# Hybrid trunk: evictions ahead of renewals in some chains, decay passes behind the cast, the dt sums one product later

## The chip, the cores and the metric

One core of one Trainium2 chip. The metric is the device time of one execution in microseconds; "before" is the median of three runs, 2637.45 us (2635.89 to 2637.7).

The engines are named as in the profile: PE (TensorE, matmuls; PEld its weight loads), DVE (VectorE), ACT (ScalarE), POOL (GpSimd) and SP (SyncE, which issues the DMAs).

## The reference

One layer of a hybrid trunk on x of 2048 tokens by 1024 channels, all in float32:

```
h = rmsnorm(x);  proj = h @ w_in          # u_b, u_c, u_h, z, xbc, dt_raw
y_a = u_b * conv3(u_c * u_h)              # short convolution mixer
xbc = silu(conv4(xbc));  dt = softplus(dt_raw + dt_bias)
y_b = chunked state-space scan over dt, a, B, C, xs   (+ d_skip * xs)
y_b = grouped rmsnorm(y_b * silu(z))
x = x + concat(y_a, y_b) @ w_out
x = x + square(relu(rmsnorm(x) @ w_up)) @ w_down;  out = rmsnorm(x)
```

In the scan each of 16 heads (two groups of eight) has within a chunk a matrix of decays exp(min(a_cum[l] - a_cum[s], 0)), which weighs the products of B and C below the diagonal.

## The kernel before

**Products.** The input projection, the MLP's up projection and its down projection are done in `chain` (L250): a two-by-two block product by seven smaller products in place of eight, in the order b11, t1, t2, b21, t3, b22, t4 (`PRODUCTS`). Each operand is held as a high and a low part of reduced width, so that each pair of blocks is three matmuls of 128x128 by 128x512 (L281 to L283). A chain with four block pairs per product has 12 matmuls per product. The accumulators lie in banks of PSUM: px and py take turns over three banks, pw has one of its own. A bank is free again when the eviction of its product has run, so a product whose bank is not yet read out waits. After b11 ACT copies px into pw (L288), and b21 adds to it.

**Evictions.** `evict` is handed in by the user of the chain. In the input projection (`Proj.pair`) s5 and s2 are copied by ACT (L746), added to later products by DVE (L749), and t4's product goes through Silu on ACT (L784); z rows are then stored to sz_d (L775, L785). In the MLP (`Mlp.pair`) they are copies, adds (L897) and squared relu (L900, L901). In the down projection (`Mlp.down`) DVE adds the product to acc (L1051).

**Renewals.** The operands of a chain are blocks uh and ul, four places of four tiles. Where the next chain needs other blocks they are renewed while the old chain runs: `fetch` or `refill` load the raw block from DRAM (rb, rh, nb), and `settle` makes the high part on ACT (L352) and the low part on DVE (L353), one place after each of t1, b21, b22 and t4. This happens in the chains of the pair z6 (the last of the first half of tokens), at the boundary of the MLP's halves and its end, and in the steps of the down projection. Weights for the next chain are loaded by SP (wraw, three buffers), combined into s12 and s34 on DVE (L214, L237), and split into whi on ACT (L100) and wlo on DVE (L101).

**Down projection.** `STEPS` (L1197): step 0 has one group of four blocks, step 1 one group of two, step 2 two groups of one and three, all later steps four blocks. The weights of step n+1 are loaded and split during step n. Before step 0 the last sums of the MLP are stored (t4, L885).

**Scan.** 32 chunks of 128 tokens by group. `front` (L1278) prepares a chunk: PE transposes xd (ptx) and B (ptb); ACT copies xtok (L1291) and btok; DVE scales xtok by decays (stmp, L1301); ACT casts the high part of it (L1303) and DVE makes the low part (L1308). Eight Relu passes (L1306, one per head) and one Exp (L1307) on ACT turn the loaded rows dec into decays. `back` then runs the products st, yo and yd. The first 16 chunks run beside the second half of the input projection with one buffer of each tile, the other 16 beside the output projection (matmuls pm, L113 to L115) with two, so that there the rows of the next chunk are loaded before the present one is through its front.

**dt.** `dt_part` (L631) is a generator that is advanced between products: pd (L640), then pt and the softplus, then after two more yields the cumulative sums pc (L677, L678), then pr and the stores of rd_d and dt_d, which the scan loads.

**Order.** Each engine runs its queue in order. The order within a queue is made when the program is built, by a scheduler that goes by the order of the code, estimated readiness and priority. `tc.high_priority(offset=n)` moves what is written in it ahead by n in priority; `tc.issue_after(i)` keeps what is written in it behind instruction i.

Of the kernel before, what the change touches and what calls it, by code (L numbers as in the profile page):

```python
# [2 lines left out]

# [1 line left out]

# [8 lines left out]
AF = mybir.ActivationFunctionType  # L14
# [10 lines left out]
G = 2  # L25
HG = 8
EPS = 1e-5
WARM = (33, 3, 6)
FF = 4096
TH = 1024  # L30
# [10 lines left out]
def trunk(ctx: ExitStack, tc: tile.TileContext, x, w_in, w_dt, w_out, w_up, w_down, cvec, hrow, out):  # L41
    nc = tc.nc
# [39 lines left out]
    eps = cv[:, NCV : NCV + 1]  # L82
    nc.vector.memset(eps, EPS)
    nc.scalar.activation(cv[:, NCV + 1 : NCV + 2], eps, AF.Sqrt)
# [39 lines left out]
    def psum(tag, name, bufs=1):  # L124
        if tag in turns:
            tag = next(turns[tag])
        return ps.tile([P, 512], F32, tag=tag, name=name, bufs=bufs)

    class Rstd:


        def __init__(self, pool, tmp, n, w):
            self.pool, self.tmp, self.scale, self.w, self.n = pool, tmp, 1.0 / n, w, w // P
# [60 lines left out]
    WHERE["b12"] = WHERE["t4"]  # L194

    class Seven:
        def __init__(self):
            self.places = [{} for _ in range(4)]

# [50 lines left out]
        def chain(self, groups, ws, ahead, evict, after):  # L250

            n = sum(len(g) for g in groups)
            pm = [{} for _ in groups]
            got = []
            seeds = self.seeds = set()
            bank = lambda acc: psum("mw" if acc == "w" else "mm", "p" + acc)
            fresh = turns.pop("fresh", ())
            if fresh:
                turns["fresh"] = fresh[1:]
            PRODUCTS = (  # L260
                ("b11", 0, 0, "x"),
                ("t1", 1, 0, "y"),
                ("t2", 1, 1, "x"),
                ("b21", 0, 1, "w"),
                ("t3", 2, 0, "x"),
                ("b22", 2, 1, "y"),
                ("t4", 3, 0, "x"),
            )
            for name, wn, half, acc in PRODUCTS:
                at = half * n  # L270
                for gi, g in enumerate(groups):
                    seeded = acc in pm[gi]
                    if not seeded:
                        pm[gi][acc] = bank(acc)
                    p = pm[gi][acc]
                    i, j = WHERE[name]
                    for k, place in enumerate(g):
                        hi, lo = (t[:, (at + k) * P : (at + k + 1) * P] for t in ws[wn])
                        h = [t[:, j] for t in place[i]]
                        kw = dict(skip_group_check=seeded)  # L280
                        nc.tensor.matmul(p, hi, h[0], start=not seeded and k == 0, stop=False, **kw)  # L281
                        nc.tensor.matmul(p, hi, h[1], start=False, stop=False, **kw)  # L282
                        nc.tensor.matmul(p, lo, h[0], start=False, stop=(k == len(g) - 1), **kw)  # L283
                    at += len(g)
                for gi in range(len(groups)):
                    if name == "b11" and not fresh:
                        pm[gi]["w"] = bank("w")
                        nc.scalar.copy(pm[gi]["w"], pm[gi]["x"])  # L288
                        seeds.add(gi)
                    evict(name, gi, pm[gi])  # L290
                if ahead is not None:
                    if name == "b11":
                        next(ahead)
                    got += take(ahead, {"b21": 2, "b22": 1, "t4": 1}.get(name, 0))
                after(name)
            return got
# [135 lines left out]
    class Proj(Seven):  # L432
# [46 lines left out]
        def begin_block(self, bb):  # L479
# [22 lines left out]
            if bb == 0:  # L502
                keep_running(WARM[1])
            st.root(bb == 0)
            yield
            r = st.spread(acc if bb else False)
            if bb == 0:
                keep_running(WARM[2])
            yield
# [121 lines left out]
        def dt_part(self, b):  # L631

            t = self.dt_tiles[b % NBB]
# [22 lines left out]
            bias = self.hb[:, 0:16].unsqueeze(1).to_broadcast([P, NC, 16])  # L656
# [16 lines left out]
            )  # L673
            yield
            yield
            pc = psum("tp", "pc", 2)
            nc.tensor.matmul(pc[:, 0:64], tri, e, start=True, stop=True)  # L677
            nc.tensor.matmul(pc[:, 64:128], ones, e, start=True, stop=True)  # L678
# [132 lines left out]
        def first_half(self, ws):  # L811
            self.last_sums()
            late = self.prepare(1, x, C_NMIX)
            for m, what in enumerate(self.PAIRS):
                last = m + 1 == len(self.PAIRS)
                if last:
                    for _ in late:
                        pass
                    ahead = self.weights(1, self.LATER[0])
                    self.new = [{} for _ in range(4)]  # L820
                else:
                    ahead = self.weights(0, self.PAIRS[m + 1])

                def after(name):
                    if name in ("b11", "b21"):
                        next(late, None)
                    if last:
                        self.refresh(name)

                ws = self.pair(0, what, ws, ahead, after)  # L830
            self.places = self.new
            return ws

        def second_half(self, ws, side):

            self.dt_weights()
            dts = itertools.chain(*(self.dt_part(NBB + bb) for bb in range(NBB)))
            for m, what in enumerate(self.LATER):
                last = m + 1 == len(self.LATER)
                ahead = self.plain(w_out[0], (0, 1)) if last else self.weights(1, self.LATER[m + 1])  # L840

                def after(name):
                    if m or name == "t4":
                        next(dts, None)
                    next(side, None)
                    if last:
                        proj_out.enter(self, name)

                ws = self.pair(1, what, ws, ahead, after)
            return ws  # L850

    class Mlp(Seven):
# [82 lines left out]
        def half(self, h, ws, late):  # L935
            for q in range(NQ):
                last = q + 1 == NQ
                if not last:
                    ahead = self.sums_of(h, q + 1)
                elif h == 0:  # L940
                    for _ in late:
                        pass
                    ahead = self.sums_of(1, 0)
                else:
                    ahead = self.weights(self.load_down(STEPS[0]))
                if last:
                    self.new = [{} for _ in range(4)]
                    if h:
                        self.own = {n: self.tmp(n) for n in ("s5", "s2", "t4")}

                def after(name):
                    if name in ("b11", "t2", "t3"):
                        next(late, None)
                    if not last:
                        return
                    if h == 0:
                        self.refresh(name)
                    else:
                        self.refill((0, 1, 2, 3), name)
                        if name == "t2":  # L960
                            self.acc = {}
                            self.outs(0, 0)

                ws = self.pair(h, q, ws, ahead, after)
            if h == 0:
                self.places = self.new
            return ws
# [50 lines left out]
        def down(self, ws):  # L1018
            late = None
            for n, step in enumerate(STEPS):  # L1020
                last = n + 1 == len(STEPS)
                ahead = self.rest_weights() if last else self.weights(self.load_down(STEPS[n + 1]))
                groups = [[self.wides[h * NQ + f] for f in fs] for h, d, fs in step]
                if not last:
# [187 lines left out]
    CHUNKS = [(b, g, c) for b in range(NB) for g in range(G) for c in range(NC)]  # L1212

    class Scan:
        def __init__(self, pool):
            self.state = []
            for g in range(G):
                s0 = pool.tile([P, 512], F32, name=f"state{g}")
                nc.vector.memset(s0, 0.0)
                self.state.append(s0)  # L1220
# [57 lines left out]
        def front(self, n):  # L1278

            b, g, c, h, ts, r0 = self.place(n)  # L1280
            t = self.got[n]
# [10 lines left out]
            hi, lo = t["btok"] = self.tile([P], "btok", 1).bitcast(F32R), bT.bitcast(F32R)  # L1292
# [7 lines left out]
                t[k] = self.tmp()  # L1300
                nc.vector.tensor_tensor(out=byhead(t[k]), in0=byhead(xtok), in1=t[by], op=ALU.mult)  # L1301
            hi, lo = t["parts"] = [a.bitcast(F32R) for a in (self.tile([512], "xtok", 1), self.tmp())]
            nc.scalar.copy(hi, t["xde"])  # L1303
            dec = t["dec"]
            for i in range(HG):
                nc.scalar.activation(dec[:, i], dec[:, i], AF.Relu, bias=t["a"][:, i : i + 1], scale=-1.0)  # L1306
            nc.scalar.activation(dec, dec, AF.Exp, scale=-1.0)  # L1307
            nc.vector.tensor_tensor(out=lo, in0=t["xde"], in1=hi.bitcast(F32), op=ALU.subtract)  # L1308
            yield
# [370 lines left out]
```

## Time and profile before

| | |
|---|---|
| median of three runs | 2637.45 us |
| the profiled execution | 2629.58 us |
| its span | 2627.8 us |
| mean granted clock of PE | 0.998 |
| DVE, ACT, POOL busy | 73%, 55%, 2% |
| chain that ended last, PE's share | 65%, and 24% "issue" |
| HBM traffic | 203 GB/s over the span |

The profiled execution lies 7.87 us under the median, 1.78 us of it outside the span. The stages lie about so in the span: input projection to 1040 us, with the first half of the scan from about 470 on; output projection with the second half of the scan to about 1330; MLP to 1990; down projection and final norm to the end. The boundary of the MLP's halves is at about 1660 to 1702.

How to read the rows: a group's row has the line, engine, operation, output and inputs, and then its times; a row of the waits says which instruction of an engine stood idle for what, with the total, the number and the longest, in us. In the timeline the first two numbers are start and duration, and brackets give the idle time before it and what ended it.

### The profile page before, as it was taken

What the parts mean: (1) busy time and instruction counts of PE and PEld (TensorE: products, weight loads), DVE (VectorE), ACT (ScalarE), POOL (GpSimd) and SP (SyncE); (2) the same over time, 40 slices, a digit from 0 to 9 for tenths busy, and PEclk for the clock granted to TensorE, in tenths of its full rate; (3) what the DMA queues carried; (4) which work ended last, traced back from release to release, by engine and by line L of the source; (5) the groups of instructions that cost most, each with busy time, mean ns of one, the idle gap of its engine ahead of it and who ended that gap; (6) DMA issues with size and microseconds to landing.
All of it is one profiled execution on the core that took longest, in us unless ns stands there. A gap on an engine that the chain in (4) does not pass through costs nothing.

```text
span 2627.8 us, 33775 instructions
## 1 busy us (share of the span) xinstructions
PE 2602.0 (99%) x12136; PEld 2140.6 (81%) x12136; DVE 1918.4 (73%) x2634; ACT 1455.3 (55%) x2211; POOL 55.7 (2%) x98
## 2 busy tenths in 40 slices
PE   9999999999999999999999999999999999999998
PEld 7888888788888888888888888888887788888887
DVE  7978867777778777878777765644448777888985
ACT  6654345776667676867336555655555444444443
POOL 0010000000000000000000000000000000000001
PEclk9999999999999999999999999999999999999999
DMA  3545745555555588877666786855558544665762
GB/s 147 203 171 192 273 144 194 190 167 172 176 167 164 165 281 255 267 225 223 201 201 235 271 311 229 285 205 206 186 200 288 154 152 151 208 213 170 247 208 77
DMA packets 252167, 536.96 MB, mean 204 GB/s; under 512 B 26208, under 2 KB 93024, under 8 KB 252000
## 3 DMA queue, kind: packets, MB, share of 16 engines
q1 hardware_dynamic: 251856, 534.29, 60.8%
q8 instruction: 95, 1.56, 0.2%
q14 instruction: 72, 0.59, 0.1%
q10 hardware_dynamic: 144, 0.52, 0.1%
HBM read 354.89 MB, written 179.83 MB: 203 GB/s over the span
## 4 chain that ended last, share of the span: by engine, by line
PE 65%; issue 24%; DMA 4%; ACT 3%; DVE 3%; SPq 0%; POOL 0%; POOLq 0%; DVEq 0%; ACTq 0%
PE px L281 10%; PE px L283 10%; PE px L282 10%; PE py L281 5%; PE py L282 5%; PE py L283 5%; PE pm L114 4%; PE pm L113 4%; PE pm L115 3%; PE pw L281 2%; PE pw L283 2%; PE pw L282 2%; DMA dec<-rd_d 1%; PE yd L1329 1%; PE yo L1326 1%
## 5 line engine op out<-in xcount | busy, mean ns | idle before, releaser
L281 PE MATMUL px<-uh,whi 128*128 128x512 f32 x1672 | 656.4, 393 | 9.6 <-DVE acc L1051 6.4
L282 PE MATMUL px<-ul,whi 128*128 128x512 f32 x1672 | 651.7, 390 | 0.0
L283 PE MATMUL px<-uh,wlo 128*128 128x512 f32 x1672 | 651.6, 390 | 0.0
L281 PEld LDWEIGHTS px<-uh,whi 128*128 128x128 f32 x1672 | 314.1, 188 | 83.7 <-DVE acc L1051 6.0
L101 DVE TENSOR_TENSOR wlo<-wraw,whi 128x1024 fp32r<-128x1024 f32 x214 | 222.6, 1040 | 202.6 <-ACT whi L100 202.5
L283 PEld LDWEIGHTS px<-uh,wlo 128*128 128x128 f32 x1672 | 314.3, 188 | 66.0 <-issue 0.2
L282 PEld LDWEIGHTS px<-ul,whi 128*128 128x128 f32 x1672 | 314.2, 188 | 63.7
L100 ACT CAST whi<-wraw 128x1024 fp32r<-128x1024 f32 x214 | 193.9, 906 | 309.3 <-PE px L282 219.2
L100 ACT CAST whi<-s 128x1024 fp32r<-128x1024 f32 x210 | 219.8, 1047 | 224.0 <-PE py L282 95.9
L281 PE MATMUL py<-uh,whi 128*128 128x512 f32 x836 | 327.1, 391 | 1.1 <-ACT eb L784 0.8
L282 PE MATMUL py<-ul,whi 128*128 128x512 f32 x836 | 325.8, 390 | 0.0
L283 PE MATMUL py<-uh,wlo 128*128 128x512 f32 x836 | 325.5, 390 | 0.0
L101 DVE TENSOR_TENSOR wlo<-s,whi 128x1024 fp32r<-128x1024 f32 x210 | 255.3, 1216 | 70.2 <-ACT whi L100 68.5
L113 PE MATMUL pm<-uh,whi 128*128 128x512 f32 (+1 forms) x648 | 250.9, 388 | 0.1
L114 PE MATMUL pm<-ul,whi 128*128 128x512 f32 (+1 forms) x648 | 248.2, 383 | 0.4 <-DVE ul L211 0.2
L115 PE MATMUL pm<-uh,wlo 128*128 128x512 f32 (+1 forms) x648 | 247.9, 383 | 0.0
L281 PEld LDWEIGHTS py<-uh,whi 128*128 128x128 f32 x836 | 157.1, 188 | 35.6 <-ACT eb L784 1.2
L283 PEld LDWEIGHTS py<-uh,wlo 128*128 128x128 f32 x836 | 156.9, 188 | 32.7
L282 PEld LDWEIGHTS py<-ul,whi 128*128 128x128 f32 x836 | 157.0, 188 | 32.3
L352 ACT CAST uh<-rh 128x1024 fp32r<-128x1024 f32 (+1 forms) x128 | 120.2, 943 | 85.3 <-PE py L283 67.2
L281 PE MATMUL pw<-uh,whi 128*128 128x512 f32 x418 | 163.3, 391 | 0.0
L283 PE MATMUL pw<-uh,wlo 128*128 128x512 f32 x418 | 162.7, 389 | 0.0
(242 smaller groups left out, 3788.4 us busy)
## 6 DMA issues: line engine op xcount, KB each, us to landing
hid_d<-e SPq DMA_DIRECT2D x96, 512.0 KB, 3.7
rh<-hid_d SPq DMA_DIRECT2D x96, 512.0 KB, 4.4
wraw<-w_in SPq DMA_DIRECT2D x68, 512.0 KB, 4.0
wraw<-w_down SPq DMA_DIRECT2D x104, 256.0 KB, 3.6
wraw<-w_up SPq DMA_DIRECT2D x48, 512.0 KB, 4.2
dec<-rd_d SPq DMA_DIRECT2D x32, 512.0 KB, 5.1
wraw<-w_out SPq DMA_DIRECT2D x32, 512.0 KB, 4.7
x_d<-xt SPq DMA_DIRECT2D x64, 256.0 KB, 3.8
```

The costliest lines, as they stand in the source:

```text
L100: nc.scalar.copy(hi, raw)
L101: eng.tensor_tensor(out=lo, in0=raw, in1=hi.bitcast(F32), op=ALU.subtract)
L113: nc.tensor.matmul(out, whi, hi, start=(k == 0), stop=False)
L114: nc.tensor.matmul(out, whi, lo, start=False, stop=False)
L115: nc.tensor.matmul(out, wlo, hi, start=False, stop=(k == nk - 1))
L281: nc.tensor.matmul(p, hi, h[0], start=not seeded and k == 0, stop=False, **kw)
L282: nc.tensor.matmul(p, hi, h[1], start=False, stop=False, **kw)
L283: nc.tensor.matmul(p, lo, h[0], start=False, stop=(k == len(g) - 1), **kw)
L352: nc.scalar.copy(p[i][0], t)
L1326: nc.tensor.matmul(yo[:, j * L : (j + 1) * L], state[:, j * P : (j + 1) * P], cT, start=True, stop=True)
L1329: nc.tensor.matmul(yd[(i % 2) * 64 : (i % 2) * 64 + 64, (i // 2) * L : (i // 2 + 1) * L], byhead(t["xdt"])[:, i, :], t["dec"][:, i % 2 * 4 ...
```

## The change

Four edits. `chain` wraps the eviction of each product in `tc.high_priority(offset=200)` where the user of the chain has set `busy`: the last pair of the first half (z6), the first pair of the second (z0), the last chain of each MLP half and the first of the second, and steps 0 to 2 of the down projection. The stores that an eviction issues are within it. In `front` the eight Relu passes are written ahead of the cast and must come after the cast of the chunk before. In `dt_part` there is one more yield ahead of pc.

```diff
...
+AHEAD = 200
...
     class Seven:
+        busy = False
...
                 for gi in range(len(groups)):
-                    if name == "b11" and not fresh:
-                        pm[gi]["w"] = bank("w")
-                        nc.scalar.copy(pm[gi]["w"], pm[gi]["x"])
-                        seeds.add(gi)
-                    evict(name, gi, pm[gi])
+                    with tc.high_priority(offset=AHEAD) if self.busy else nullcontext():
+                        if name == "b11" and not fresh:
+                            pm[gi]["w"] = bank("w")
+                            nc.scalar.copy(pm[gi]["w"], pm[gi]["x"])
+                            seeds.add(gi)
+                        evict(name, gi, pm[gi])
...
             yield
             yield
+            yield
             pc = psum("tp", "pc", 2)
...
             for m, what in enumerate(self.PAIRS):
-                last = m + 1 == len(self.PAIRS)
+                self.busy = last = m + 1 == len(self.PAIRS)
...
                 last = m + 1 == len(self.LATER)
+                self.busy = m == 0
...
             for q in range(NQ):
                 last = q + 1 == NQ
+                self.busy = last or (h == 1 and q == 0)
...
                 last = n + 1 == len(STEPS)
+                self.busy = n < 3
...
     class Scan:
+        cast = None
+
...
-            nc.scalar.copy(hi, t["xde"])
             dec = t["dec"]
-            for i in range(HG):
-                nc.scalar.activation(dec[:, i], dec[:, i], AF.Relu, bias=t["a"][:, i : i + 1], scale=-1.0)
+            with tc.issue_after(self.cast.ins) if self.cast else nullcontext():
+                for i in range(HG):
+                    nc.scalar.activation(dec[:, i], dec[:, i], AF.Relu, bias=t["a"][:, i : i + 1], scale=-1.0)
+            self.cast = nc.scalar.copy(hi, t["xde"])
             nc.scalar.activation(dec, dec, AF.Exp, scale=-1.0)
```

In the order of ACT in the second half of the scan, before (dec are the decay rows of the next chunk, xtok and stmp those of the present one, ry and whi belong to the output projection):

```order
L1306 ACTIVATE dec_9565<-dec_9565,dd_9558 128x128 x5
L1348 ACTIVATE stmp_9618<-y_9427 128x512
L1291 COPY xtok_9592<-ptx_9584 128x512
L1293 CAST btok_9594<-ptb_9589 128x128
L1311 ACTIVATE xd_9374<-xd_9374,cv_154 128x128 x4
L1306 ACTIVATE dec_9565<-dec_9565,dd_9558 128x128 x3
L1458 ACTIVATE ry_10310<-ry_10310,cv_154 128x512
L1303 CAST xtok_9651<-stmp_9647 128x512
L1307 ACT_TABLE_LOAD
L1307 ACTIVATE dec_9565<-dec_9565 128x1024
```

And now:

```order
L1359 ACTIVATE stmp_9618<-y_9427 128x512
L1322 ACTIVATE xd_9374<-xd_9374,cv_154 128x128
L1301 COPY xtok_9592<-ptx_9584 128x512
L1303 CAST btok_9594<-ptb_9589 128x128
L1322 ACTIVATE xd_9374<-xd_9374,cv_154 128x128 x3
L1317 CAST xtok_9651<-stmp_9647 128x512
L1316 ACTIVATE dec_9565<-dec_9565,dd_9558 128x128 x7
L101 CAST whi_9817<-wraw_9815 128x1024
L1316 ACTIVATE dec_9565<-dec_9565,dd_9558 128x128
L1469 ACTIVATE ry_10312<-ry_10312,cv_154 128x512
L1318 ACT_TABLE_LOAD
L1318 ACTIVATE dec_9565<-dec_9565 128x1024
```

The cast of the present chunk (L1303, now L1317) stood behind all eight passes of the next chunk and now stands ahead of them; the passes, the table load and the exponential follow it.

In the order of DVE at the end of down step 2, before (px_17233 is the bank of t4's first group here, acc_17140 its sum; s12, s34 and the raw wraw are weights of the next step, rh and ul renewed blocks):

```order
L214 TENSOR_TENSOR s12_17313<-s12_17313,wraw_17251 128x512
L1051 TENSOR_TENSOR acc_17136<-px_17233,acc_17136 128x512
L1051 TENSOR_TENSOR acc_17143<-px_17237,acc_17143 128x512
L1051 TENSOR_TENSOR acc_17139<-py_17259,acc_17139 128x512
L101 TENSOR_TENSOR wlo_17317<-s12_17313,whi_17316 128x1024
L1051 TENSOR_TENSOR acc_17146<-py_17263,acc_17146 128x512
L214 TENSOR_TENSOR s34_17354<-wraw_17251,wraw_17252 128x512
L214 TENSOR_TENSOR s34_17354<-wraw_17251,s12_17313 128x512
L353 TENSOR_TENSOR ul2_17362<-rh_17324,uh2_17361 128x1024
L1051 TENSOR_TENSOR acc_17140<-px_17233,acc_17140 128x512
L101 TENSOR_TENSOR wlo_17358<-s34_17354,whi_17357 128x1024
L1051 TENSOR_TENSOR acc_17146<-px_17237,acc_17146 128x512
```

And now:

```order
L217 TENSOR_TENSOR s12_17313<-s12_17313,wraw_17251 128x512
L357 TENSOR_TENSOR ul1_17321<-rh_17279,uh1_17320 128x1024
L1059 TENSOR_TENSOR acc_17146<-py_17263,acc_17146 128x512
L1059 TENSOR_TENSOR acc_17140<-px_17233,acc_17140 128x512
L102 TENSOR_TENSOR wlo_17317<-s12_17313,whi_17316 128x1024
L1059 TENSOR_TENSOR acc_17146<-px_17237,acc_17146 128x512
L217 TENSOR_TENSOR s34_17354<-wraw_17251,wraw_17252 128x512
L217 TENSOR_TENSOR s34_17354<-wraw_17251,s12_17313 128x512
L357 TENSOR_TENSOR ul2_17362<-rh_17324,uh2_17361 128x1024
L357 TENSOR_TENSOR ul3_17386<-rh_17365,uh3_17385 128x512
L102 TENSOR_TENSOR wlo_17358<-s34_17354,whi_17357 128x1024
L102 TENSOR_TENSOR wlo_17382<-wraw_17252,whi_17381 128x512
```

The eviction into acc_17140 stood behind the split of s12, another eviction, two sums and the settle ul2, and now stands ahead of all but that other eviction.

In the order of DVE at the pair z6, before (eb and ea take t3 and b22, rb and ul are blocks for the second half):

```order
L353 TENSOR_TENSOR ul1_3700<-rb_3651,uh1_3699 128x1024
L101 TENSOR_TENSOR wlo_3692<-s12_3688,whi_3691 128x1024
L353 TENSOR_TENSOR ul1_3704<-rb_3653,uh1_3703 128x1024
L353 TENSOR_TENSOR ul1_3708<-rb_3655,uh1_3707 128x1024
L749 TENSOR_TENSOR eb_3590<-px_3591,s5_3631 128x512
L749 TENSOR_TENSOR ea_3589<-py_3618,s2_3669 128x512
L101 TENSOR_TENSOR wlo_3752<-s34_3748,whi_3751 128x1024
L353 TENSOR_TENSOR ul2_3756<-rb_3711,uh2_3755 128x1024
L353 TENSOR_TENSOR ul2_3760<-rb_3713,uh2_3759 128x1024
```

And now:

```order
L357 TENSOR_TENSOR ul1_3700<-rb_3651,uh1_3699 128x1024
L102 TENSOR_TENSOR wlo_3692<-s12_3688,whi_3691 128x1024
L754 TENSOR_TENSOR eb_3590<-px_3591,s5_3631 128x512
L357 TENSOR_TENSOR ul1_3704<-rb_3653,uh1_3703 128x1024
L357 TENSOR_TENSOR ul1_3708<-rb_3655,uh1_3707 128x1024
L754 TENSOR_TENSOR ea_3589<-py_3618,s2_3669 128x512
L102 TENSOR_TENSOR wlo_3752<-s34_3748,whi_3751 128x1024
L357 TENSOR_TENSOR ul2_3756<-rb_3711,uh2_3755 128x1024
L357 TENSOR_TENSOR ul2_3760<-rb_3713,uh2_3759 128x1024
```

The eviction of t3 (L749, now L754) has gone ahead of two settles, that of b22 stays behind them. On PE, t4 of z6 and of z0 now follows b22 directly; before, five matmuls of the next chain's b11 stood between. At the start of step 0 the whole b11 of that step stood ahead of the MLP's last t4 and now stands behind it, and in step 0 t3 is now before b22. On SP, one load of acc that stood between the last store of the MLP (L885) and the weights of step 1 (L981) now stands ahead of the store, and the store of sz_d for t4 of z6 (L785) stands ahead of the last loads of rb.

More of the change, by code (lines that the diff above doesn't have):

```diff
@@ L1 @@
 import itertools
-from contextlib import ExitStack
+from contextlib import ExitStack, nullcontext
 import numpy as np
```

## The prediction

> **What bounds the kernel now.** I read the page first (busy time, chain), then the waits of TensorE (PE), then the timelines of the places where PE waits.
>
> ```profile
> span 2627.8 us, 33775 instructions
> ...
> PE 2602.0 (99%) x12136; PEld 2140.6 (81%) x12136; DVE 1918.4 (73%) x2634; ACT 1455.3 (55%) x2211; POOL 55.7 (2%) x98
> ```
>
> PE is busy for 2602.0 of 2627.8 us. The change removes no matmul, so it can only take from the 25.8 us in which PE stands still, and from time that PE is busy but slow. The waits of PE say for whom it stands:
>
> ```profile
> PE px L281 <- DVE acc L1051: 6.4, 6, 2.9
> ...
> PE st L113 <- ACT xtok L1303: 1.3, 2, 0.9
> ...
> PE st L114 <- DVE stmp L1308: 1.1, 3, 0.6
> PE py L281 <- ACT eb L784: 0.8, 1, 0.8
> PE px L281 <- ACT s L746: 0.7, 1, 0.7
> ...
> PE px L281 <- DVE eb L749: 0.5, 1, 0.5
> ```
>
> Columns: us in total, times, longest. The same view cut to 1990 to 2050 us, the first steps of the down projection, holds most of the first row:
>
> ```profile
> PE px L281 <- DVE acc L1051: 5.1, 3, 2.9
> ```
>
> Matmul records run over each other, so an idle gap understates a stop. PE's timeline around the longest one:
>
> ```profile
> 2039.11 0.47 PE L281 MATMUL px<-uh,whi 128*128 128x512 f32 x1 [2.90 <-DVE acc L1051]
> ...
> 2040.13 0.63 PE L282 MATMUL px<-ul,whi 128*128 128x512 f32 x1
> ...
> 2043.52 0.40 PE L281 MATMUL py<-uh,whi 128*128 128x512 f32 x1
> ...
> 2046.31 0.39 PE L281 MATMUL px<-uh,whi 128*128 128x512 f32 x1
> 2046.53 0.39 PE L282 MATMUL px<-ul,whi 128*128 128x512 f32 x1
> ```
>
> At full speed a matmul lasts 0.39 us and the next starts 0.22 to 0.23 us after it, so every stop costs about 0.16 us more than the idle gap: this one 2.90 + 0.16 = 3.06. It costs more still. From 2040.13 to 2043.52 PE starts eight matmuls, 0.42 us apart in place of 0.226: 8 x 0.2 = 1.6 us. The windows show why:
>
> ```profile
> 2040.00:2042.00 2.00, 2.00 (x7) 1.56 (x6) 2.00 (x5) 0.00 (x0) 0.00 (x0) 0.52 0.77 270
> 2042.00:2044.00 2.00, 2.00 (x8) 1.55 (x6) 1.70 (x3) 0.28 (x1) 0.00 (x0) 0.63 0.86 227
> ```
>
> The third number from the end is the granted clock: about half speed for some 3.4 us from 2040.1 on. The stop is worth 3.1 + 1.6 = 4.7 us.
>
> [...]
>
> **The change part by part.**
>
> *Down steps.* Why did the bank wait? DVE (VectorE) at the end of step 2:
>
> ```profile
> 2034.20 1.23 DVE L101 TENSOR_TENSOR wlo<-s,whi 128x1024 fp32r<-128x1024 f32 x1 [0.15 <-ACT whi L100]
> 2035.34 0.68 DVE L1051 TENSOR_TENSOR acc<-py,acc 128x512 f32<-128x512 f32 x1
> ...
> 2038.28 0.68 DVE L1051 TENSOR_TENSOR acc<-px,acc 128x512 f32<-128x512 f32 x1
> ```
>
> The eviction of t4's first group runs at 2038.28, behind a split, an eviction, two sums and a settle, all done without a gap. In the changed order it stands right behind the b22 eviction, ahead of the split of s12: PE stops at 2036.05 (2039.11 - 3.06), and t4's second group is nine matmuls, 2.0 us, so the first group was through at 2034.0. Evicted at once, it leaves its bank by about 2035, while PE is still busy with the second. The stop goes: -4.7. The split moves back by 1.2 us (two evictions at 0.6 apart) but feeds t1, which starts twelve matmuls (2.7 us) after b11.
>
> In step 0 two stops go as well: 5.1 - 2.9 = 2.2 idle, with 0.3 for the records 2.5 us. But step 1 needs weights. SyncE (SP), then ScalarE (ACT):
>
> ```profile
> 1999.20 0.32 SPq L885 DMA_DIRECT2D hid_d<-t  x1
> ...
> 2000.52 1.94 SPq L981 DMA_DIRECT2D wraw<-w_down  x4
> ```
>
> ```profile
> 2005.24 0.62 ACT L100 CAST whi<-wraw 128x512 fp32r<-128x512 f32 x1 [7.40 <-DMA wraw<-w_down]
> ```
>
> The weights are issued behind the store of t4's block, which waits for a DVE subtraction. In the changed order three evictions (0.6 each) come ahead of that subtraction, and the settles they overtake go behind it; one load that stood between the store and the weights now stands ahead of the store (about -0.45). I take the weights 0.3 us later (0 to 1.3). So PE reaches step 1 about 2.5 us sooner and waits there: the 2.5 is given back, and 0.3 with it: net +0.3.
>
> *The pair chains z6 and z0 (450 to 475 us).* Three stops: eb L749 0.5, eb L784 0.8, s L746 0.7, with 0.16 each 2.5 us. The evictions ran late behind other work:
>
> ```profile
> 452.78 2.35 DVE L353 TENSOR_TENSOR ul<-rb,uh 128x1024 fp32r<-128x1024 f32 x2
> 455.05 0.68 DVE L749 TENSOR_TENSOR eb<-px,s 128x512 f32<-128x512 f32 x1
> ```
>
> ```profile
> 460.57 0.59 ACT L784 ACTIVATE eb<-px 128x512 f32<-128x512 f32 x1
> ```
>
> The first now precedes these two settles, so it can run at 452.8, 2.3 us sooner, where the stop it caused is 0.5 long. The second can run sooner by what t4 comes sooner and by what ACT did ahead of it; I leave 0.4 us of its stop, half of it, since ACT may be within a cast (the settles there take 1 us each): -2.1. Stores belonging to an eviction move with it: sz_d's second store now stands on SP ahead of the last loads of rb, which then wait for the eviction; these loads feed the fourth block, used only by t4. POOL's queue is unchanged.
>
> *The decay passes (1040 to 1330 us).* PE's stops for xtok and stmp: 1.3 + 1.1 idle in five, with 5 x 0.16: 3.2 us. One of them on ACT:
>
> ```profile
> 1090.08 1.57 ACT L1306 ACTIVATE dec<-dec,dd 128x128 f32<-128x128 f32 x5 [2.48 <-DMA dec<-rd_d]
> ...
> 1093.89 0.98 ACT L1306 ACTIVATE dec<-dec,dd 128x128 f32<-128x128 f32 x3
> 1094.77 0.71 ACT L1458 ACTIVATE ry<-ry,cv 128x512 f32<-128x512 f32 x1
> 1095.38 0.61 ACT L1303 CAST xtok<-stmp 128x512 fp32r<-128x512 f32 x1
> ```
>
> The eight passes before this cast are those of the next chunk; the first five even waited for that chunk's rows while this chunk's copies stood behind. Now they come after the cast, which gains 1.57 + 0.98 us and most of the 2.48 wait: 2.5 to 5 us, against a longest stop of 0.9 + 0.16. The subtraction L1308 follows the cast, so its stops go too. What is added: the passes, a table load and the exponential stand as one block of 8 x 0.3 + 1.3 + 1.1 = 4.8 us, with weight casts behind it. No PE row names a weight cast in this stage, so it has cover now; if the cover is gone, that is up to 2.4 us (the passes) a chunk. I take -3.2.
>
> *The dt sums.* pc and what follows it (pr, the stores of rd_d and dt_d) come one product, 12 x 0.226 = 2.7 us, later; the scan reads what they store chunks later. No row of PE's waits names pc or pr, and the smallest rows there are 0.2: 0, bounds -0.2 to +0.3.
>
> *New small stops.* Orders that were re-sorted elsewhere (470 to 560 us, the products around each eviction) will hit some bank or cast a little late. The nearest rows are stops like eb L749's, 0.5 + 0.16; I take two: +1.3 (0 to 3).
>
> Sum: -4.7 + 0.3 - 2.1 - 3.2 + 1.3 = -8.4 us. The profiled execution took 2629.58 us (span 2627.8 and 1.8 around it), 7.9 below the median of the runs, 2637.45; I take the same difference from both: 2621.2 profiled, 2629.0 median.
>
> **The rivals.** 0.2% (5.3 us) is about what a measurement of this kernel can tell from no change.
>
> 1. *Step 0's gain is kept.* If the weights come sooner than I think (the load moved ahead of the store, less traffic), the 2.5 + 0.3 isn't given back: -8.4 - 2.8 = -11.2, 2626.2. Against: the four loads took 4 us each to land, and the cast waited 7.40 us for them.
> 2. *The clock falls at step 1.* The two stops of step 0 become one of about 2.5 to 3 us before b11 of step 1, near the 2.9 that halved the clock. Price up to 1.6; with the weights at their late bound (+1.0) and the small stops at theirs (+1.7): -8.4 + 4.3 = -4.1, 2633.3. [...]
> 3. *The scan doesn't gain.* The casts come early, but the stops pass to the weight casts or the exponential behind the unbroken block: -8.4 + 3.2 = -5.2, and with one more 0.9 + 0.16 stop -4.1, 2633.3 again.
> 4. *Slower: evictions block DVE.* An eviction placed early waits for its product, and settles and splits behind it wait too, up to one product (2.7 us). DVE takes its queue in order: the rows at 2034 to 2039 show it. It decides where PE needs a settle less than 2.7 us after it was due. Around the boundary of the MLP halves PE has no gap to give:
>
> ```profile
> 1660.00:1702.00 42.00, 42.00 (x185) 34.43 (x184) 34.15 (x40) 34.84 (x50) 0.00 (x0) 1.00 0.89 318
> ```
>
> If the three MLP chains and the three down steps each lose one product, that is +16.2 in place of the down steps' -4.4, so -8.4 + 4.4 + 16.2 = +12.2: 2649.7. Against: the order puts most evictions only one to three places ahead.
> 5. *It changes nothing measurable* (each stop is replaced by one next to it): 2637.
>
> **How the numbers follow.** Chances: forecast 0.47, rival 1 0.10, rivals 2 and 3 0.15 each, rival 4 0.09, rival 5 0.04. Faster by over 0.2%: nearly all of the forecast (0.43), rival 1, and a quarter of 2 and 3 (0.08): 0.61. Slower: rival 4 and a tail, 0.10. Within: 0.29. Low end: rival 1 with no new small stops (-11.2 - 1.3 = -12.5), 2625.0. High end: rival 5, 2637.5; beyond it lie rival 4 and half of 5. The forecast's own range is 2626.5 to 2632.
>
> **What would show it.** In the changed profile: no wait on acc before step 3 and a clock of 1.00 at 2040 us; a wait on whi of 2 to 3.5 us at step 1 in place of two on acc; no PE wait on xtok from 1040 to 1330; the three stops at 450 to 475 gone but for some tenths. I am wrong if PE waits on wlo or ul in the MLP or steps 1 to 3, or if the scan's stops only change their name.

## The result and the profile after

| | before | after |
|---|---|---|
| median, 20 runs each on one chip | 2637.04 us (2632.69 to 2642.9) | 2632.11 us (2628.05 to 2639.11) |
| ratio, 95% interval | | 0.9985 (0.9979 to 0.9991) |
| again on another chip, 15 and 11 runs | 2637.91 us | 2630.78 us, ratio 0.9973 (0.9964 to 0.9982) |
| the profiled execution, its span | 2629.58, 2627.8 us | 2632.07, 2629.7 us |

By the ratio the kernel became faster by 4.0 us (0.0015 x 2637; the interval makes it 2.4 to 5.5), and by 7.1 us (4.7 to 9.5) the second time. The forecast was 2629.0 in a range of 2625.0 to 2637.5: the sign and the range held, the sum of -8.4 was about twice the first result. One of the 11 runs of the second timing took 6537.49 us at a mean clock of 0.392 and is left out of the ratio.

The two profiled executions, on the other hand, stand 2.5 us the wrong way round. The one of before is a lucky one: 2629.58 us lies below the lowest of the 20 runs, 2632.69. So the profiles are compared here by place, and never by their ends. First the head of the page after:

```profile
span 2629.7 us, 33771 instructions
...
PE 2604.8 (99%) x12136; PEld 2143.3 (82%) x12136; DVE 1920.1 (73%) x2634; ACT 1461.4 (56%) x2215; POOL 55.7 (2%) x98
```

PE stands still for 24.9 us (25.8 before), but is busy 2.8 us longer with the same matmuls, and ACT has four instructions more (2211 before). Where this lies shows in the windows by stage. Columns: stretch, its length, busy time of PE, PEld, DVE, ACT, POOL with instructions, PE's granted clock, DMA share, GB/s. Before:

```profile
440.00:480.00 40.00, 37.96 (x172) 30.44 (x171) 30.02 (x36) 31.01 (x50) 0.00 (x0) 1.00 0.85 270
480.00:560.00 80.00, 79.97 (x411) 61.67 (x410) 57.77 (x115) 64.09 (x108) 1.36 (x5) 1.00 0.53 171
1040.00:1330.00 290.00, 287.57 (x1486) 237.73 (x1485) 225.83 (x347) 177.77 (x333) 0.00 (x0) 1.00 0.74 231
1990.00:2060.00 70.00, 64.59 (x272) 51.30 (x271) 57.30 (x80) 26.95 (x37) 0.00 (x0) 0.98 0.71 230
2060.00:2600.00 540.00, 538.63 (x2388) 444.15 (x2387) 431.55 (x551) 232.95 (x276) 0.00 (x0) 1.00 0.56 178
```

The same windows after:

```profile
440.00:480.00 40.00, 39.55 (x181) 31.98 (x180) 31.14 (x38) 32.22 (x49) 0.00 (x0) 1.00 0.85 283
480.00:560.00 80.00, 76.25 (x378) 58.03 (x377) 55.69 (x109) 62.91 (x106) 2.58 (x4) 0.96 0.51 158
1040.00:1330.00 290.00, 289.24 (x1499) 240.11 (x1498) 224.80 (x345) 183.69 (x343) 0.00 (x0) 1.00 0.75 234
1990.00:2060.00 70.00, 66.55 (x283) 53.47 (x283) 58.29 (x79) 28.35 (x37) 0.00 (x0) 0.98 0.75 243
2060.00:2600.00 540.00, 537.13 (x2372) 441.74 (x2371) 431.29 (x548) 231.43 (x272) 0.00 (x0) 1.00 0.56 178
```

Length less PE's busy time is PE's idle time: 2.04 us before and 0.45 after in z6 and z0; 2.43 and 0.76 in the second half of the scan; 5.41 and 3.45 in the first down steps. These are the three places where the forecast saw a gain. Against them stand 1.37 and 2.87 in the later down steps, and one place that the forecast had at nothing: from 480 to 560 us PE stood still for 0.03 us and now for 3.75. Its waits there, after (before, PE has none of these four):

```profile
PE st L114 <- ACT xtok L1317: 1.3, 1, 1.3
PE pc L682 <- DVE dts L675: 0.9, 1, 0.9
PE yo L1337 <- DVE state L1350: 0.8, 1, 0.8
PE st L115 <- DVE stmp L1319: 0.7, 1, 0.7
```

And the granted clock after, in windows of 2 and 4 us, behind these waits and in the first down steps:

```profile
542.00:544.00 2.00, 1.14 (x2) 0.42 (x2) 1.46 (x3) 1.97 (x3) 0.00 (x0) 0.68 0.81 216
544.00:546.00 2.00, 1.46 (x7) 1.46 (x8) 1.62 (x2) 1.99 (x3) 0.00 (x0) 0.50 0.84 273
546.00:548.00 2.00, 2.00 (x13) 1.46 (x12) 1.29 (x2) 1.82 (x6) 0.00 (x0) 0.50 1.03 333
548.00:550.00 2.00, 2.00 (x7) 1.61 (x7) 0.00 (x0) 0.00 (x0) 0.00 (x0) 0.61 0.46 119
...
2010.00:2012.00 2.00, 2.00 (x6) 1.10 (x6) 1.69 (x5) 0.81 (x2) 0.00 (x0) 0.61 1.01 311
2012.00:2014.00 2.00, 2.00 (x6) 1.53 (x7) 1.47 (x3) 1.21 (x3) 0.00 (x0) 0.53 0.95 276
...
2036.00:2040.00 4.00, 4.00 (x20) 3.30 (x19) 4.00 (x7) 2.63 (x3) 0.00 (x0) 1.00 0.16 26
2040.00:2044.00 4.00, 4.00 (x19) 3.32 (x18) 4.00 (x6) 1.30 (x2) 0.00 (x0) 1.00 0.38 134
```

Before step 3, at 2036 to 2044, PE is busy throughout at a clock of 1.00: the stop of 2.90 and the half clock behind it are gone. At step 1 the clock now falls instead, which costs 2.00 x 0.39 + 2.00 x 0.47 = 1.7 us; worked out so from the two windows that the prediction shows, the fall at 2040 in before cost 2.00 x 0.48 + 2.00 x 0.37 = 1.7 too. At 542 to 550 a fall is new: 1.14 x 0.32 + 1.46 x 0.50 + 2.00 x 0.50 + 2.00 x 0.39 = 2.9 us. With 3.72 us more of idle, the place from 480 to 560 costs 6.6 us more than before, and the 2.9 are about the 2.8 us by which PE is busy longer.

### The profile page after: what moved, and what is told of

The parts are those of the page before. It is cut to its first block, busy times and chain, and to the rows that moved or that the text cites. A ratio compares the mean times of both kernels' runs of the same rounds, so it can differ in the third digit from the quotient of the medians.

```text
span 2629.7 us, 33771 instructions
## 1 busy us (share of the span) xinstructions
PE 2604.8 (99%) x12136; PEld 2143.3 (82%) x12136; DVE 1920.1 (73%) x2634; ACT 1461.4 (56%) x2215; POOL 55.7 (2%) x98
## 4 chain that ended last, share of the span: by engine, by line
PE 88%; DMA 4%; DVE 3%; issue 2%; ACT 2%; SPq 0%; POOL 0%; POOLq 0%; DVEq 0%; ACTq 0%
PE px L284 13%; PE px L285 13%; PE px L286 13%; PE py L284 6%; PE py L285 6%; PE py L286 6%; PE pm L114 5%; PE pm L115 5%; PE pm L116 5%; PE pw L284 3%; PE pw L286 3%; PE pw L285 3%; PE yd L1340 1%; PE yo L1337 1%; DMA wraw<-w_down 1%
## 5 line engine op out<-in xcount | busy, mean ns | idle before, releaser
L102 DVE TENSOR_TENSOR wlo<-wraw,whi 128x1024 fp32r<-128x1024 f32 x214 | 222.5, 1040 | 208.6 <-ACT whi L101 208.4
L102 DVE TENSOR_TENSOR wlo<-s,whi 128x1024 fp32r<-128x1024 f32 x210 | 255.3, 1216 | 72.6 <-ACT whi L101 71.2
```

Of the source, the lines that this page charges most:

```text
L102: eng.tensor_tensor(out=lo, in0=raw, in1=hi.bitcast(F32), op=ALU.subtract)
```

## The experiments

**One edit at a time.** My theory was the forecast's: the gain is the evictions' and the decay passes', and the yield in the dt chain is worth nothing. The rival: the dt yield is what takes the rest of the gain away. The first three kernels hold one edit each, the fourth all but the yield.

The decay passes alone (e1):

```diff
-            nc.scalar.copy(hi, t["xde"])
             dec = t["dec"]
-            for i in range(HG):
-                nc.scalar.activation(...)
+            with tc.issue_after(self.cast.ins) if self.cast else nullcontext():
+                for i in range(HG):
+                    nc.scalar.activation(...)
+            self.cast = nc.scalar.copy(hi, t["xde"])
```

> The decay passes behind the cast alone, of the whole change. Both theories expect the stops of TensorE for xtok and stmp between 1040 and 1330 us to go, as they mostly did in the changed kernel: about -2.8 us against before (ratio 0.9989), 87 table loads on ScalarE as before.

Measured: 0.9981 (0.9971 to 0.9991), 5.0 us faster. The evictions alone (e2), without the edits to `front` and `dt_part`:

> The evictions ahead alone. Theory D (the later dt sums make ScalarE change tables more often and cost some 6 us at 520 to 550 us): this kernel has no such loss, so -2.0 at 450 to 475 us and -3.0 in the down steps: -5 us (ratio 0.998), no TensorE wait on xtok at 540 us. Rival B (the pulled evictions of z0 and after push the scan's work at 540 us back): the loss is here, so +1 us, and the waits on pc, xtok and stmp at 520 to 550 us appear.

Measured: 0.9987 (0.9979 to 0.9996), 3.4 us faster. PE has no wait at 480 to 560 us there (0.03 us idle), so rival B, by which the evictions make the loss, falls. The yield alone (e3):

```diff
             yield
             yield
+            yield
             pc = psum("tp", "pc", 2)
```

> The dt sums one product later alone. Theory D: two table loads more than before (89), waits of TensorE on pc, xtok or stmp at 520 to 550 us, +3 to +6 us (ratio 1.001 to 1.0023). Rival B: no change, within 1 us of before.

Measured: 1.0009 (0.9999 to 1.0018), 2.4 us slower, just within what could still be no change, and less than the +3 to +6 expected. It makes 89 table loads, and PE is idle for 1.78 us at 480 to 560. And everything but the yield (e4, the changed kernel with two yields there):

> The change without the later dt sums (evictions ahead and decay passes, both as in the changed kernel). Theory D: the loss at 520 to 550 us is gone, -8 us against before (ratio 0.997), faster than the changed kernel by 4 us. Rival B: as the changed kernel, -4 us (0.9985).

Measured: 0.9962 (0.9951 to 0.9974), 10.0 us faster than before. So the evictions and the decay passes together give about what they give apart (5.0 + 3.4 = 8.4 of 10.0), and with the yield 3 to 6 us of it are lost: 7.1 us left in the one timing of the changed kernel, 4.0 in the other. In e4 the place of the loss is whole, PE busy from end to end:

```profile
480.00:560.00 80.00, 80.00 (x411) 62.13 (x410) 59.37 (x118) 64.81 (x114) 2.46 (x5) 1.00 0.54 169
```

The 6.6 us of that place in the profile after are near the 6 us between e4's ratio and the changed kernel's first (0.0023 x 2637). Against its second ratio it is only 2.9 us (0.0011 x 2637), so how much of the place's loss reaches the whole time is not settled.

e2 and e3 also show how much the scan's stops vary, since both lack the decay edit. PE's waits from 1040 to 1330 us in e2:

```profile
PE st L114 <- ACT xtok L1312: 3.5, 2, 2.9
```

and in e3:

```profile
PE st L114 <- ACT xtok L1312: 4.5, 2, 3.5
```

These executions of the old order stop for up to 3.5 us for the cast where before's profile showed 0.9. It is the same stop, at 1208 us in before, 1212 in e2 and 1216 in e3, with the same order of ACT ahead of it. With the edit, in e1, one stop of this kind is left, of 1.0 (e5 and e6 have some of up to 1.2):

```profile
PE st L115 <- DVE stmp L1317: 1.0, 1, 1.0
```

**Why does one yield cost so much?** What stands behind it shows in ACT's timeline. After:

```profile
519.74 0.70 ACT L1316 ACTIVATE dec<-dec,dd 128x128 f32<-128x128 f32 x2 [1.88 <-DMA dec<-rd_d]
...
530.95 0.60 ACT L765 ACTIVATE ea<-pw 128x512 f32<-128x512 f32 x1
531.56 1.28 ACT L697 ACT_TABLE_LOAD   x1
532.86 0.27 ACT L697 ACTIVATE dts<-pr 64x128 f32<-64x128 f32 x1
...
533.62 1.28 ACT L773 ACT_TABLE_LOAD   x1
...
540.16 0.69 ACT L1316 ACTIVATE dec<-dec,dd 128x128 f32<-128x128 f32 x2
540.76 0.60 ACT L1317 CAST xtok<-stmp 128x512 fp32r<-128x512 f32 x1
541.38 1.28 ACT L1318 ACT_TABLE_LOAD   x1
542.67 1.06 ACT L1318 ACTIVATE dec<-dec 128x1024 f32<-128x1024 f32 x1
543.74 1.28 ACT L789 ACT_TABLE_LOAD   x1
545.04 0.60 ACT L789 ACTIVATE eb<-px 128x512 f32<-128x512 f32 x1
```

e4, with two yields, the same work:

```profile
517.82 1.87 ACT L1315 ACTIVATE dec<-dec,dd 128x128 f32<-128x128 f32 x6 [0.44 <-DMA dec<-rd_d]
...
521.00 0.70 ACT L1315 ACTIVATE dec<-dec,dd 128x128 f32<-128x128 f32 x2
521.72 1.28 ACT L1317 ACT_TABLE_LOAD   x1
523.01 1.06 ACT L1317 ACTIVATE dec<-dec 128x1024 f32<-128x1024 f32 x1
...
529.55 0.26 ACT L696 ACTIVATE dts<-pr 64x128 f32<-64x128 f32 x1
...
537.79 0.61 ACT L1316 CAST xtok<-stmp 128x512 fp32r<-128x512 f32 x1
538.31 0.59 ACT L788 ACTIVATE eb<-px 128x512 f32<-128x512 f32 x1
```

In these rows each turn from an exponential to a Silu or back is a table load of 1.28 us, and takes little more of ACT's time than that: in the profile after the Silu L765 ends at 531.55 us, the load of L697 starts at 531.56, and the exponential behind it at 532.86. In e4 the dt exponentials (the last is L696) follow each other, and the exponential of the decays (L1317) is over at 524. With the third yield a Silu (L765) comes between the dt exponentials, with a load behind it, and the chunk's decay passes are torn apart: the first two waited 1.88 us for the rows of rd_d, which pr stores, and the last two with their exponential stand at 540 to 544, between Silus, with a load on either side. For the same work ACT makes eight loads after, from L689 to L789, and six in e4; two more extra loads stand ahead of these, from 490 us on. In the whole kernel it makes 87 before and in e4, 91 after. ACT is full there (busy 25.28 of the 26 us from 520 to 546), so the cast of xtok, the Silu behind it and what DVE does with them are late, and PE with them.

Theory D: it is the place of the dt exponentials among the Silus that costs, by the loads. The rival L: it is that they are later, for whoever waits for the sums. Five yields in place of two (e5) are later still, one in place of two (e6) is earlier:

> The change with the dt sums three products later still (five yields ahead of pc; the changed kernel has three, before two). The number of table loads on ScalarE falls back from 91 to 87. Theory D (the loss comes from the table loads, by where the dt exponentials fall among Silu): no loss at 520 to 550 us, as without the later sums, ratio 0.996 (-10 us). Rival L (lateness itself costs, through the dt rows and what waits for them): the loss stays or grows, 0.9985 or more.

> The change with the dt sums one product earlier than before (one yield). 89 table loads. Theory D: about half of the loss comes back, though the sums are earlier: +2 to +3 us against the change without later sums, ratio about 0.997. Rival L: no loss, 0.996.

Measured: e5 0.9958 (0.9944 to 0.9971) with 87 loads, e6 0.9967 (0.9955 to 0.998) with 89. The place in e5:

```profile
480.00:560.00 80.00, 79.56 (x411) 62.28 (x410) 60.19 (x118) 64.94 (x113) 1.80 (x5) 1.00 0.55 170
```

and in e6, where one product *earlier* brings the stops and a lower clock back:

```profile
480.00:560.00 80.00, 78.08 (x391) 59.57 (x390) 55.51 (x110) 63.39 (x107) 2.17 (x4) 0.98 0.53 165
```

So L falls: three products later costs nothing at the place (0.44 us idle), and no time in all. That e6 is slower than e5 as a whole is not resolved, the intervals overlap. The loads alone were then put in (e10): e4 with four exponentials of one column, whose output nothing uses, behind Silus of z4:

```diff
+                        if h == 1 and what == "z4":
+                            nc.scalar.activation(self.probe, to["c11"][:, 0:1], AF.Exp, scale=0.0)
```

> The change without later dt sums, plus four one-column exponentials on ScalarE, one behind each Silu of the pair z4 of the second half (520 to 550 us); what they compute is not used. They bring three more table loads (90 in place of 87) and 0.8 us of their own. Theory D (table loads at this place cost TensorE its time, not the order of the dt work): 2 to 5 us slower than without them (ratio to before 0.997 to 0.998), with TensorE waits on xtok or stmp at about 540 us. Rival O (what costs is that the dt work itself comes later, on VectorE): no change, 0.996, no such waits.

Measured: 0.9964 (0.9951 to 0.9976), 90 loads. At the place PE stops for the cast of xtok again, with no dt step moved:

```profile
PE st L114 <- ACT xtok L1325: 1.9, 1, 1.9
PE py L284 <- ACT eb L795: 0.5, 1, 0.5
```

The stage behaves as D says, 2.6 us idle and a clock of 0.98; the whole time doesn't show it against e4, where I expected 2 to 5 us. Over all versions PE's idle time from 480 to 560 us goes with the loads of the kernel: 0.00 to 0.62 us in the nine executions with 87 loads, 1.78 and 1.92 with 89 (e3, e6), 2.55 with 90 (e10), and 3.75 in both with 91. D is shown for the place, and the price of the yield for the whole kernel; that all of that price is the loads is inferred from the two.

**What is the wait at step 1 of the down projection?** In the changed kernel and in e4 PE waits for whi there, 3.4 and 4.1 us at a time, where before had two waits for acc, 2.2 us together. The forecast says step 0's gain is given back. e7 takes the early evictions of steps 0 and 1 back; those of the MLP's last chain stay ahead:

```diff
-                self.busy = n < 3
+                self.busy = n == 2
```

> The change without later dt sums, and in the down projection the evictions go ahead in step 2 alone. Theory W (what steps 0 and 1 gain is given back as a wait for the weights of step 1, and the one long wait slows the clock): the two stops on acc in step 0 come back (2.5 us), the wait on whi at step 1 (4.3) falls to 0.5 and the clock stays at full speed there; -2 us against the change without later sums. The stop on acc before step 3 stays away. Rival G (step 0's gain is kept): slower by 2.5 us than the change without later sums.

Measured: 0.996 (0.9948 to 0.9972), as e4. PE's waits from 1990 to 2060 us in e7:

```profile
PE px L284 <- ACT whi L101: 2.5, 1, 2.5
PE px L284 <- DVE acc L1058: 1.2, 1, 1.2
```

Together 3.7; e4 has 4.1 and another 0.5 for acc. Evictions sooner in step 0 move the stop to the weights and gain nothing that the time shows. I had expected only 0.5 for whi and a clock at full speed; it falls to 0.50 behind the 2.5. Why whi comes so much later than in before (0.3) was not tried; the MLP's evictions are what still differs. Is it the transfer or its place in SP's queue? e8 puts the issue of step 1's weights ahead, e9 step 2's also:

```diff
-                            nc.sync.dma_start(r[:, b, at : at + len(fs)], w_down[d, 2 * i + b, ...])
+                            with tc.high_priority(offset=20) if step in STEPS[1:3] else nullcontext():
+                                nc.sync.dma_start(r[:, b, at : at + len(fs)], w_down[d, 2 * i + b, ...])
```

(e9; in e8 `step is STEPS[1]`.)

> The change without later dt sums, and the loads of step 1's weights are issued by SyncE ahead of the last stores of the MLP. Theory W: the wait of TensorE on whi at step 1 (4.3 us and a slower clock after it) goes, -4 to -5 us against the change without later sums (ratio to before about 0.9945). Rival T (the transfers themselves set the time, the queue not): the wait stays within 1 us of 4.3, or the renewed blocks come late in its place; no gain.

Measured for e8: 0.9961 (0.9949 to 0.9973), as e4 and not the 4 to 5 us faster that I expected. Step 1's wait is gone, and one of 3.7 us stands before step 2, whose weights are issued behind eleven loads of acc (SP's timeline; the second number is the time that issuing took):

```profile
1997.24 6.50 SPq L1015 DMA_DIRECT2D acc<-x_d  x11
2003.78 2.50 SPq L988 DMA_DIRECT2D wraw<-w_down  x2
```

> As the run with step 1's weights loaded early, and step 2's weights are issued ahead of eight of the loads of acc as well. Theory Q (SyncE's order of loads sets the wait: whatever weights stand behind the loads of acc come late): the 3.7 us wait of TensorE at step 2 goes too, and the slower clock with it: -4 to -5 us against the change without later sums (ratio to before about 0.9945). Rival T (the sum of the transfers from 1990 to 2012 us sets it): the wait moves on once more, to step 3's weights or to acc, and stays above 2 us in all.

Measured for e9: 0.9955 (0.9941 to 0.9968), 2624.73 us, the lowest median of the versions with more than one run. The weights now go after three of these loads, and the stage keeps its clock:

```profile
1996.95 2.96 SPq L1015 DMA_DIRECT2D acc<-x_d  x3
1999.96 3.75 SPq L988 DMA_DIRECT2D wraw<-w_down  x8
```

```profile
1990.00:2060.00 70.00, 68.08 (x300) 55.75 (x299) 59.51 (x83) 27.74 (x35) 0.00 (x0) 1.00 0.72 241
```

PE's idle time there is 1.92 us, 3.45 in the changed kernel and 4.63 in e4. The order of the issues made the waits for weights. A wait of 1.9 us in all, for acc, is left in the stage, 1.8 of it at 2009 us, so part of the wait has moved on, as rival T had it, but to just under the 2 us that it named. The gain of 4 to 5 us on e4 that I expected did not show: e4's and e9's intervals overlap for the most part.

e11 tests the clock: e4 with fourteen matmuls without use behind step 0.

```diff
+                if n == 0:
+                    keep_running(14)
```

> The change without later dt sums, plus 14 idle matmuls on TensorE (3.1 us, result unused) between step 0's t4 and step 1's b11, inside the wait of 4.1 us for weights. Theory C (the clock falls because TensorE stands idle): the granted clock from 2000 to 2012 us stays at 1.00 and no matmul there takes 0.42 us; the wait shrinks to about 1 us and step 1 starts no later. Rival: the clock falls there all the same.

Measured in one run: 2622.79 us, too few to rank it. But the wait for whi shrinks from 4.1 to 0.5 us, and the clock holds where e4's falls. e4:

```profile
2004.00:2006.00 2.00, 2.00 (x5) 1.45 (x6) 1.69 (x5) 0.62 (x1) 0.00 (x0) 0.50 0.99 318
2006.00:2008.00 2.00, 2.00 (x7) 1.27 (x6) 1.13 (x3) 1.41 (x3) 0.00 (x0) 0.67 0.91 309
```

and e11:

```profile
2004.00:2006.00 2.00, 1.50 (x6) 0.59 (x5) 1.69 (x5) 1.50 (x4) 0.00 (x0) 1.00 0.92 293
```

So, by one execution of each, it is PE's idleness that lowers the clock there. Last, the changed kernel a second time beside these (e12):

> The changed kernel as it is, on the same chip as the others of this call. Theory D: waits of TensorE on pc, xtok and stmp at 520 to 550 us again, of 3 us or more in all; 5 to 6 us slower than the change without later sums (0.9985 to before). Rival (that stop was an accident of the one profile): no such waits.

Measured: 0.9973 (0.9964 to 0.9982), and the same four waits at 480 to 560 us, to a tenth. Against e4's ratio this is 2.9 us slower, where I expected 5 to 6. The loss at that place belongs to the kernel, not to an execution.

## Why the prediction was right, and where it was not

- *The stop before step 3 and its half clock, -4.7.* Right: PE runs through at a clock of 1.00 in the profile after.
- *Step 0 and 1, given back, +0.3.* The gain was given back, as the step said, but its size was off. One wait of 3.4 us took the place of 2.2 us of idle, and the clock fell behind it, which is rival 2. The two windows of the down steps give the sum: idle time 5.41 to 3.45, one fall of the clock in each, so -2.0 us for a forecast of -4.7 + 0.3 = -4.4. This term was +2.7 in place of +0.3. In e12 the same wait was 2.8 us and the clock held, so 1.7 of it come and go.
- *z6 and z0, -2.1.* Measured in the windows: -1.6.
- *The decay passes, -3.2.* About right, in part by luck. Measured alone it is -5.0, with an interval (2.4 to 7.6) that holds 3.2. The term took all the stops of one execution, which lay under all timed runs, and let none remain. PE's idle time from 1040 to 1330 us is 2.43, 5.25 and 5.44 us in the three executions of the old order (before, e2, e3) and 0.00 to 3.67 in the eleven of the new, 4.4 and 1.4 in the mean: the old order stops for longer than I took, and the new one keeps some stops. Rival 3, no gain in the scan, fell.
- *The dt sums, 0, bounds -0.2 to +0.3.* This is the step that failed. I asked who on PE waits for pc, found no one, and left it there. I never followed the three exponentials that move with pc through ACT's queue. They cost +2.4 alone and 3 to 6 us in company, ten to twenty times my bound. What the runs show in place of the 0 are table loads on a full ACT: four more loads of 1.28 us each, and 6.6 us lost by PE where they stand. What made the difference between "alone" and "in company" was not tried by itself; e3 makes two loads more than before, the changed kernel four, and in e3, too, PE waits for xtok there, but its clock stays at 1.00.
- *New small stops, +1.3.* About right: 1.5 us more idle in the later down steps.
- *Rival 4, slower by evictions that block DVE.* Nothing of it was seen; the evictions alone are 3.4 us faster.

The sum without the dt edit, -8.4, stands against a measured -10.0 (6.9 to 12.9); with it, -4.0 and -7.1. So the forecast's sum stands without the dt step, and that step took back what no rival had foreseen. That the range held all the same is in part luck: it reached up to 2637.5 for other reasons (rivals 2, 3 and 5), and the first median, 2632.11, lies just beyond the forecast's own range of 2626.5 to 2632. Where all of e4's 10.0 us lie is not shown, since the windows are those of a profiled execution of before that is 7.5 us faster than its median. The version to keep is the change without the yield, with the early weights or without.

## What to carry to other kernels

A moved step has to be followed on every engine that it touches: count the table loads in ACT's order before and after (here 87 and 91, of 1.28 us each), above all where ACT is full (here 25.28 of 26 us). Before a gain is sized from a stop, see whether the profiled execution is near the median, and take a second execution's stops where it isn't. Removing the stop ahead of a transfer can move the stop to the transfer: in e4 it did, and PE's idle time in that stage fell from 4.63 to 1.92 us only when the transfers moved ahead in their queue (e9).

## What the runs showed of the hardware

The clock fell after as little as 2.5 us of idleness. In the first down steps one idle time of 2.5 us (e7) was followed by half clock, as were 2.9 (before, e1, e3), 3.4 (after) and 4.1 (e4); after 2.4 (e10) and 2.8 (e12) it stayed at 1.00, as it did after the 2.9 us in the scan of e2. So between 2.5 and 2.9 us it went either way in these executions. Nor did it take a single long gap: at 540 to 543 us in the profile after, PE stops for 1.31 and 0.71 us with little work between, and from 542.7 on, worked out from the window's 0.68, the clock stands at 0.50; a third stop, of 0.78, falls into the slow stretch.

What a fall in the down steps cost was 1.7 us in before, after and e4 (there 2.00 x 0.50 + 2.00 x 0.33), whatever the idle time ahead of it. It is not a constant: in e3, behind the same 2.9 us, the windows of 2 us from 2046 to 2054 have clocks of 0.69, 0.50, 0.50 and 0.60, which is 6.8 us at half clock in place of 3.4, and costs about 3.0 us; the mean clock from 1990 to 2060 us is 0.95 there, and 0.98 in before, after and e4. The fall at 542 us in the profile after, with 0.68, 0.50, 0.50 and 0.61, is as long.
